# Mixer products on the un-normalised operand, weight subtractions on VectorE, and chunk decay at the state's copy

## The chip, the cores and the metric

The kernel runs on one core of a Trainium2 chip. The core has a matrix engine (TensorE, PE in the profile; its weight loads are shown as PEld), VectorE (DVE), ScalarE (ACT), GpSimd (POOL) and SyncE (SP, which here only issues transfers). Every engine works through its own queue in order and waits on semaphores for the others. Matrix products land in PSUM; all else lives in the on-chip SBUF or in DRAM. The metric is the device time of one execution in microseconds (us).

## The reference

One layer of a hybrid block on 512 tokens of width 1024, all in float32:

```python
x = x + 0.5 * swiglu(rms_norm(x, ffn1_norm), ffn1_w1, ffn1_w3, ffn1_w2)
h = rms_norm(x, mix_norm)
p = h @ w_in                       # all columns of both mixers and the gates
y_a = rwkv7_mixer(token_shift(p[rwkv columns])) @ rwkv_proj
y_b = fox_mixer(p[fox columns]) @ fox_proj
x = x + (sigmoid(g_a) * y_a + sigmoid(g_b) * y_b) @ w_out
x = x + 0.5 * swiglu(rms_norm(x, ffn2_norm), ffn2_w1, ffn2_w3, ffn2_w2)
out = rms_norm(x, final_norm)
```

`rms_norm` multiplies each token by one number, 1/sqrt(mean(x*x)+eps), and each column by a gain. The RWKV mixer is a recurrence over tokens with a 64x64 state in each of 8 heads: S_t = S_{t-1} diag(w_t) + (S_{t-1} a_t) b_t^T + v_t k_t^T, y_t = S_t r_t. The FoX mixer is causal attention with 8 heads, RMS norm of q and k per head, and a cumulative log-forget bias. The last lines of the RWKV mixer are a norm over each head (group norm), a bonus term and a gate g.

## The kernel before

**Layout.** Activations are kept transposed: 8 tiles xT of 128 columns by 512 tokens. So the normalising number of a token, rstd, is a row; it is held as a 128x512 tile, the same in every partition. Every float32 product is made from three matmuls of a split operand: each side is cut into a rounded part (hi) and a rest (lo), and hi·hi, hi·lo and lo·hi are summed in PSUM (`mm3`, L121 to L123). `cols` (L205) makes one product of 128 columns: 8 pieces of the 1024-long sum, 24 matmuls of 128x128 by 128x512.

**Weights.** `load_raw` (L100) fetches a 128-column slice with a transfer on SP's queue, into three rotating buffers. `split_w` (L107) has ScalarE round it (whi, L113) and another engine subtract (wlo, L114), each into two rotating buffers. The fifth argument picks the engine of the subtraction: VectorE where nothing is said, GpSimd where `pool` is passed. Before, `pool` is passed for the mixer's k, r and v (L471, L475, L479), q and k of FoX (L709) and the gates (L741).

**Norm.** In the feed-forward stages the operand carries only the gain and rstd is multiplied in when the product leaves PSUM (L331, L335). The mixer's first two products (psa and psg, L412, L413: low-rank codes, forget logits and the g codes) do the same (L420, L424). Then `rescale` (L196) rewrites all eight operand tiles with gain and rstd in place, splits them again, and every later product is of the normalised operand.

**Stages of the mixer.** (1) For each of four pairs of heads p, the products of k, r and v, the token shift (`shifted`, L403, a ScalarE scaling and a VectorE multiply-add), decays by a scan in chunks of 32 tokens (L484), the normalised kk with a sum over each head by a matmul (`headsum`, L130), and the operands G and BK of the chunked recurrence. GpSimd makes the products of r with the decay (L520), kk times a (L512) and BKe (L521), which is BK times the decay to the end of its chunk. (2) The inverse of a unit triangular 32x32 matrix for each of 16 chunks in each of 8 heads: 31 steps of two VectorE instructions (L569, L571). (3) A trip of its result through DRAM (Td, L572 and L578) to the layout that the recurrence needs. (4) The recurrence over 16 chunks c: xps (L622), copied as Xs (L625), ups (L629), copied into the right-hand side R (L631, L632), sps (L636), the next state, copied to the next R (L637, L638), and the output yps (L644). sps multiplies R with D, which holds BKe transposed and a diagonal block with the decay of the chunk, made by GpSimd (L610, in `stage`). Between these small products TensorE runs q and k of FoX (`load_qk`, L704), the attention and the first gates (`gate`, L739, called by `early`). (5) The group norm (L661 to L683). (6) The output projections.

**Order.** The kernel is written against tiles; a scheduler at build time orders the instructions on each engine. `holes` is written by hand: it lists matmuls of the recurrence behind which single pieces of a gate's product are put. Memory of each pool is set out by tags: a tile with the tag of another takes its place.

Of the kernel before, what the change touches and what calls it, by code (L numbers as in the profile page):

```python
# [18 lines left out]
P = 128  # L19
# [31 lines left out]
def kernel(  # L51
# [77 lines left out]

    def headsum(ps, src, hi=None, lo=None):  # L130
        hi = tmp("shi", dt=F32R)[:] if hi is None else hi
        lo = tmp("slo", dt=F32R)[:] if lo is None else lo
        dve.tensor_copy(hi, src)
        dve.tensor_tensor(lo, src, hi.bitcast(F32), op=ALU.subtract)
        pe.matmul(ps, bonesr[:], hi, start=True, stop=False)
        pe.matmul(ps, bonesr[:], lo, start=False, stop=True)
# [13 lines left out]
    class Norm:  # L150
# [36 lines left out]
        def finish(s):  # L187
# [6 lines left out]
            act.activation(s.rstd[:], ln[:], AF.Exp, scale=-0.5)  # L194

        def rescale(s, c):  # L196
            t = xT[c]
            dve.scalar_tensor_tensor(t[:], xT[c][:], pc(s.gain + c), s.rstd[:], op0=ALU.mult, op1=ALU.mult)
            hi = xp.tile([P, T], F32R, tag=f"xh{c}", name=f"xh{c}")
            lo = xp.tile([P, T], F32R, tag=f"xl{c}", name=f"xl{c}")  # L200
            act.copy(hi[:], t[:])
            (pool if c % 2 else dve).tensor_tensor(lo[:], t[:], hi[:].bitcast(F32), op=ALU.subtract)
            s.hi[c], s.lo[c] = hi, lo

# [179 lines left out]
    with ExitStack() as mx:  # L384
# [4 lines left out]
        G = [[sp.tile([P, NC, 2, C], F32, name=f"G{p}{q}", tag=f"G{p}{q}") for q in range(2)] for p in range(NP)]  # L389
        BKe = [sp.tile([P, NC, 2, C], F32, name=f"BKe{p}", tag=f"BKe{p}") for p in range(NP)]  # L390

# [25 lines left out]
        lg = rp.tile([P, T], F32, name="lg")  # L417
        fz = la
        u = tmp("u")
        dve.tensor_tensor(u[0:72, :], psa[0:72, :], mix.rstd[0:72, :], op=ALU.mult)  # L420
        shifted(la, u, 64, PAR_MUA)
        dve.tensor_scalar(fz[64:72, :], u[64:72, :], pc(PAR_F)[64:72, :], None, op0=ALU.add)
        u = tmp("u")
        dve.tensor_tensor(u[0:96, :], psg[0:96, :], mix.rstd[0:96, :], op=ALU.mult)  # L424
# [10 lines left out]
        dve.tensor_tensor(lx[q2], la[q1, :], f32(lx[q1]), op=ALU.subtract)  # L435
        zslots = [h for g in G[3] for h in (g[:, 0:8], g[:, 8:16])] + [BKe[3][:, 0:8], BKe[3][:, 8:16]]
        zslots = [h.rearrange("p c a t -> p (c a t)") for h in zslots] + spare[0:2]
# [31 lines left out]
        for p in range(NP):  # L469
            kps = bank("pk")  # L470
            mix.cols(kps[:], *load_w(win(DA + p * P), KD, P, pool), P)  # L471
            k = prep("k", p)
            shifted(k, kps, P, PAR_MU + 4 + p)
            rps = bank("pk")
            mix.cols(rps[:], *load_w(win(p * P), KD, P, pool), P)  # L475
            r = prep("r", p)
            shifted(r, rps, P, PAR_MU + p)
            vps = bank("pk")
            mix.cols(vps[:], *load_w(win(2 * DA + p * P), KD, P, pool), P)  # L479
            v = vs[p]  # L480
            shifted(v, vps, P, PAR_MU + 8 + p)

# [18 lines left out]
            ps = bank("pn", pf)  # L501
            headsum(ps[:], sq[:])
            rn = tmp("krn")
# [10 lines left out]
            dve.tensor_tensor(BK[:, :, 0, :], ch(ka), ch(Pi), op=ALU.mult)  # L514
            dve.tensor_tensor(BK[:, :, 1, :], ch(k), ch(Pi), op=ALU.mult)
            for q in range(2):
                s = slice(q * 64, (q + 1) * 64)
                dve.scalar_tensor_tensor(G[p][q][s, :, 0, :], ch(kk)[s], -1.0, Pp[s, :, 0:C],
                                         op0=ALU.mult, op1=ALU.mult)
# [70 lines left out]
        for q in range(2):  # L590
            pool.memset(Rs[0][half(q), :, q, :], 0.0)
            for i in range(4):
                o = (1 - q) * 64
                pool.memset(Rs[i][o:o + 32, :, q, :], 0.0)

        def stage(c):
            vp = pr.tile([P, NP, 2, 64], F32, tag="b", name="vp")
            for p in range(NP):
                pe.transpose(vp[0:64, p].rearrange("p a b -> p (a b)"), vs[p][:, c * C:(c + 2) * C], ident[:])
            bp = pr.tile([P, NP, 2, 64], F32, tag="b", name="bp")  # L600
            for p in range(NP):
                pe.transpose(bp[:, p].rearrange("p a b -> p (a b)"),
                             BKe[p][:, c:c + 2].rearrange("p c a b -> p (c a b)"), ident[:])
            for j in range(2):
                Rj, Dj = Rs[(c + j) % 4], Ds[(c + j) % 4]
                for q in range(2):
                    o = 32 + (1 - q) * 64
                    act.copy(Rj[o:o + 32, :, q, :], vp[j * C:(j + 1) * C, :, q, :])
                    act.copy(Dj[half(1 - q), :, q, :], bp[half(j), :, q, :])
                    pool.tensor_tensor(Dj[half(q), :, q, :],  # L610
                                       ident[half(q), half(q)].unsqueeze(1).broadcast_to([64, NP, 64]),
                                       PC[half(q), :, c + j:c + j + 1].broadcast_to([64, NP, 64]), op=ALU.mult)

        stage(0)

        for c in range(NC):
# [16 lines left out]
            if c + 1 < NC:  # L633
                sps = pr.tile([P, NP, 64], F32, tag="b", name="sps")
                for p, q in heads():
                    hs = pe.matmul(sps[half(q), p, :], Dt[:, p, q, :], R[:, p, q, :], start=True, stop=True)  # L636
                dve.tensor_copy(Rn[0:64, :, 0, :], sps[0:64])  # L637
                dve.tensor_copy(Rn[64:128, :, 1, :], sps[64:128])  # L638
            holes += [hx, hu, hu, hs]
# [12 lines left out]
        tslot = [Tall[:, i * T:(i + 1) * T] for i in range(4)]  # L652
        ya = [duo(f"BKe{p}", f"ya{p}", F32R) for p in range(NP)]
# [3 lines left out]
        nc.sync.dma_start(gup[0:96, :], rwkv_g_up[0])  # L657
        bons = gslot[12:16]
        for p in range(NP):
# [44 lines left out]
        def load_qk(p):  # L704
            both = []
            for c0, par0 in ((COL_Q, PAR_Q), (COL_KF, PAR_K)):
                o = t2.tile([P, T], F32, name=f"qk{c0}{p}")
                ps = bank("pq")
                mix.cols(ps[:], *load_w(win(c0 + p * P), KD, P, pool), P,  # L709
                         holes if 2 * p + (c0 == COL_KF) >= 7 else ())  # L710
# [3 lines left out]
                both.append((o, sq))  # L714
            for o, sq in both:
                ps = bank("pq2", pf)
                headsum(ps[:], sq[:])
# [16 lines left out]
        for b in range(NB):  # L734
            o = t2.tile([P, T], F32, name=f"vt{b}") if b else xp.tile([P, T], F32, tag="rstd", name="vt0")
# [211 lines left out]
```

## Time and profile before

| | us |
|---|---|
| median of 3 runs | 1253.06 |
| lowest, highest | 1250.62, 1253.21 |
| profiled execution | 1249.56 |
| its span, first to last instruction | 1247.5 |
| TensorE busy in the span | 1198.1 |
| VectorE, ScalarE, GpSimd busy | 673.6, 451.9, 232.6 |

The profile is of one execution. A row of a group has the line of the code, the engine, the operation, what is written and read, shapes, the count, then the time that the group kept its engine busy, the mean duration of one in nanoseconds, and the idle time of the engine right before these instructions with what ended it. A row of a stretch has its start and end, its length, and for each engine the busy time and the number of instructions. A row of a wait has who waited for whom, the total, the number of times, and the longest. A row in order of time has the start, the duration and the instruction. The clock is that granted to TensorE, 1.00 being full. Matmuls overlap with their neighbours, so the duration of one is longer than the time from one start to the next.

### The profile page before, as it was taken

How to read it: one execution, taken by the hardware profiler on the slowest of the kernel's cores; microseconds unless marked ns; L12 is line 12 of the kernel's file. 1: busy time of each engine (PE TensorE's matmuls, PEld its weight loads, DVE VectorE, ACT ScalarE, POOL GpSimd, SP SyncE). 2: the span in 40 equal slices, each digit the busy share in tenths (PEclk: the TensorE clock that was granted, in tenths of full speed). 3: DMA queues.
4: the chain of work that ended last, by engine and by line, in shares of the span. 5: the costliest groups of instructions: out<-in, count | busy, mean ns of one | idle time of the engine just before them, and what ended most of it. 6: DMA issues, size and time to landing. Idle time of an engine off the chain costs nothing.

```text
span 1247.5 us, 15857 instructions
## 1 busy us (share of the span) xinstructions
PE 1198.1 (96%) x6336; PEld 963.8 (77%) x6336; DVE 673.6 (54%) x930; ACT 451.9 (36%) x722; POOL 232.6 (19%) x202
## 2 busy tenths in 40 slices
PE   8999999999997999969889999999999999999997
PEld 6888888888884777757666777778888888888887
DVE  7544555433337788984655446487455454443332
ACT  6222222222224733436766557233322222222221
POOL 4100000001114576443221132233000000000110
PEclk9999999999998999989989999999999999999999
DMA  6233333333332233332120153543333323333332
GB/s 191 85 102 101 93 94 101 96 102 110 110 103 76 68 90 84 98 96 57 44 75 27 52 161 127 169 126 94 92 94 102 99 87 101 102 93 93 92 89 73
DMA packets 210231, 120.04 MB, mean 96 GB/s; under 512 B 11790, under 2 KB 202318, under 8 KB 210158
## 3 DMA queue, kind: packets, MB, share of 16 engines
q1 hardware_dynamic: 208382, 113.26, 31.0%
q0 software_dynamic: 1760, 5.77, 1.4%
q8 instruction: 50, 0.82, 0.3%
q14 instruction: 23, 0.19, 0.0%
q10 hardware_dynamic: 16, 0.00, 0.0%
HBM read 109.58 MB, written 9.44 MB: 95 GB/s over the span
## 4 chain that ended last, share of the span: by engine, by line
PE 84%; DVE 12%; ACT 2%; issue 1%; DMA 1%; SPq 0%; POOL 0%; DVEq 0%; ACTq 0%
PE pd L123 7%; PE pd L121 7%; PE pd L122 7%; PE pb L123 6%; PE pa L123 6%; PE pa L122 6%; PE pa L121 6%; PE pb L122 6%; PE pb L121 6%; PE pgt L121 3%; PE pgt L122 2%; PE pgt L123 2%; DVE prod L569 2%; PE pk L122 1%; PE pw L123 1%
## 5 line engine op out<-in xcount | busy, mean ns | idle before, releaser
L113 ACT CAST whi<-raw 128x1024 fp32r<-128x1024 f32 (+3 forms) x199 | 198.3, 997 | 629.0 <-PE pa L122 178.8
L114 DVE TENSOR_TENSOR wlo<-raw,whi 128x1024 fp32r<-128x1024 f32 (+2 forms) x162 | 192.7, 1190 | 115.9 <-ACT whi L113 113.9
L123 PE MATMUL pb<-xh,wlo 128*128 128x512 f32 x344 | 134.1, 390 | 0.9 <-DVE wlo L114 0.9
L121 PE MATMUL pa<-xh,whi 128*128 128x512 f32 x344 | 134.8, 392 | 0.0
L121 PE MATMUL pb<-xh,whi 128*128 128x512 f32 x344 | 134.4, 391 | 0.0
L123 PE MATMUL pa<-xh,wlo 128*128 128x512 f32 x344 | 134.1, 390 | 0.0
L122 PE MATMUL pa<-xl,whi 128*128 128x512 f32 x344 | 134.0, 390 | 0.0
L122 PE MATMUL pb<-xl,whi 128*128 128x512 f32 x344 | 134.0, 390 | 0.0
L123 PE MATMUL pd<-hh,wlo 128*128 128x512 f32 x330 | 131.3, 398 | 0.0
L121 PE MATMUL pd<-hh,whi 128*128 128x512 f32 x330 | 130.4, 395 | 0.0
L122 PE MATMUL pd<-hl,whi 128*128 128x512 f32 x330 | 130.4, 395 | 0.0
L114 POOL TENSOR_TENSOR wlo<-raw,whi 128x1024 fp32r<-128x1024 f32 x37 | 91.6, 2475 | 125.4 <-ACT whi L113 123.6
L335 DVE TENSOR_TENSOR fb<-pb,rstd 128x512 f32<-128x512 f32 x43 | 29.7, 691 | 137.2 <-PE pb L123 137.2
L123 PEld LDWEIGHTS pb<-xh,wlo 128*128 128x128 f32 x344 | 64.6, 188 | 14.7 <-DVE wlo L114 1.3
L121 PEld LDWEIGHTS pa<-xh,whi 128*128 128x128 f32 x344 | 64.6, 188 | 13.8 <-issue 0.5
L122 PEld LDWEIGHTS pb<-xl,whi 128*128 128x128 f32 x344 | 64.6, 188 | 13.6 <-issue 0.2
L121 PEld LDWEIGHTS pb<-xh,whi 128*128 128x128 f32 x344 | 64.6, 188 | 13.7 <-ACT whi L113 0.3
L122 PEld LDWEIGHTS pa<-xl,whi 128*128 128x128 f32 x344 | 64.6, 188 | 13.6 <-issue 0.2
L123 PEld LDWEIGHTS pa<-xh,wlo 128*128 128x128 f32 x344 | 64.6, 188 | 13.4
L899 POOL TENSOR_TENSOR facc<-facc,osq 128x512 f32<-128x512 f32 x6 | 10.1, 1676 | 346.6 <-ACT osq L898 346.6
L122 PEld LDWEIGHTS pd<-hl,whi 128*128 128x128 f32 x330 | 62.0, 188 | 14.9
L123 PEld LDWEIGHTS pd<-hh,wlo 128*128 128x128 f32 x330 | 62.0, 188 | 14.8 <-issue 0.2
(359 smaller groups left out, 2154.1 us busy)
## 6 DMA issues: line engine op xcount, KB each, us to landing
raw<-in_ffn_w_dram SPq DMA_DIRECT2D x118, 512.0 KB
raw<-in_w_in_dram SPq DMA_DIRECT2D x40, 512.0 KB
raw<-in_ffn_w_dram SPq DMA_DIRECT2D x15, 384.0 KB
raw<-in_w_out_dram SPq DMA_DIRECT2D x8, 512.0 KB
gsave<-gs SPq DMA_DIRECT2D x12, 256.0 KB
xin<-in_x_dram SPq DMA_DIRECT2D x4, 512.0 KB
xsave<-xT POOLq DMA_DIRECT2D x8, 256.0 KB, 2.3
ga<-gsave SPq DMA_DIRECT2D x8, 256.0 KB
```

Of the source, the lines that this page charges most:

```text
L113: act.copy(hi[:], raw[:])
L114: (eng or dve).tensor_tensor(lo[:], raw[:], hi[:].bitcast(F32), op=ALU.subtract)
L121: pe.matmul(ps, whi, xhi, start=first, stop=False)
L122: pe.matmul(ps, whi, xlo, start=False, stop=False)
L123: pe.matmul(ps, wlo, xhi, start=False, stop=last)
L335: dve.tensor_tensor(b[:], pb[:], nrm.rstd[:], op=ALU.mult)
L569: dve.tensor_tensor(pv, TT[:, 0:n, t:t + 1].broadcast_to([P, n, m]), Lu[:, t, n:C].unsqueeze(1).broadcast_to([P, n, m]), op=ALU.mult)
L899: pool.tensor_tensor(acc[:], acc[:], sq[:], op=ALU.add)
```

## The change

Six things change; the rest follows from them.

1. `rescale` goes. All products of the mixer are of the operand with the gain alone. A product is multiplied by rstd on VectorE as it leaves PSUM: k, r and v in a new function `normed`, q and k of FoX and the gates in place. The attention's v has its tokens in partitions, so it needs rstd as a column: four transposes of rstd give `rc`, and ScalarE's copy of v takes it as a scale. The gain of q and k moves to the last multiplication of these.
2. The weight subtractions of the mixer that were on GpSimd are on VectorE.
3. kk times a and the products of r with the decay move from GpSimd to VectorE.
4. BKe goes. The transposes in `stage` read BK itself, which is kept for all four p; the diagonal block of D is a plain identity, written once; and the decay of the chunk is multiplied into the state by VectorE as it leaves PSUM, in place of two copies.
5. `headsum` takes its rounded part from ScalarE for the norms of k (RWKV) and of q and k (FoX).
6. rstd stays alive longer, so v's first tile has a place of its own, and the g codes (lg) are a temporary tile that is stored to DRAM and fetched again in the group norm.

```diff
-    def headsum(ps, src, hi=None, lo=None):
+    def headsum(ps, src, hi=None, lo=None, eng=None):
...
-        dve.tensor_copy(hi, src)
+        if eng is act:
+            act.copy(hi, src)
+        else:
+            dve.tensor_copy(hi, src)
...
-        def rescale(s, c):
-            t = xT[c]
-            dve.scalar_tensor_tensor(t[:], xT[c][:], pc(s.gain + c), s.rstd[:], op0=ALU.mult, op1=ALU.mult)
...
-            act.copy(hi[:], t[:])
-            (pool if c % 2 else dve).tensor_tensor(lo[:], t[:], hi[:].bitcast(F32), op=ALU.subtract)
...
-        for c in range(KD):
-            mix.rescale(c)
+        rc = rp.tile([P, NB], F32, name="rc")
+        rps = bank("rct", pr)
+        for b in range(NB):
+            pe.transpose(rps[:, b * P:(b + 1) * P], mix.rstd[:, b * P:(b + 1) * P], ident[:])
+        dve.tensor_copy(rc[:], rps[:, 0:T:P])
...
+        def normed(ps, rows=P):
+            u = tmp("u")
+            dve.tensor_tensor(u[0:rows, :], ps[0:rows, :], mix.rstd[0:rows, :], op=ALU.mult)
+            return u
...
+        nc.sync.dma_start(lgsave[:], lg[0:96, :])
...
-            mix.cols(kps[:], *load_w(win(DA + p * P), KD, P, pool), P)
+            mix.cols(kps[:], *load_w(win(DA + p * P), KD, P), P)
             k = prep("k", p)
-            shifted(k, kps, P, PAR_MU + 4 + p)
+            shifted(k, normed(kps), P, PAR_MU + 4 + p)
...
-            headsum(ps[:], sq[:])
+            headsum(ps[:], sq[:], eng=act)
...
-            pool.tensor_tensor(ka[:], kk[:], a[:], op=ALU.mult)
-            BK = t2.tile([P, NC, 2, C], F32, name="BK", tag="BK", bufs=2)
+            dve.tensor_tensor(ka[:], kk[:], a[:], op=ALU.mult)
+            BK = BKs[p]
...
-                pool.tensor_tensor(G[p][q][s, :, 1, :], ch(r)[s], Pp[s, :, 1:C + 1], op=ALU.mult)
-            pool.tensor_tensor(BKe[p][:].rearrange("p c a t -> p c (a t)"),
-                              BK[:].rearrange("p c a t -> p c (a t)"),
-                              Pp[:, :, C:C + 1].broadcast_to([P, NC, 2 * C]), op=ALU.mult)
+                dve.tensor_tensor(G[p][q][s, :, 1, :], ch(r)[s], Pp[s, :, 1:C + 1], op=ALU.mult)
...
+                pool.tensor_copy(Ds[i][half(q), :, q, :],
+                                 ident[half(q), half(q)].unsqueeze(1).broadcast_to([64, NP, 64]))
...
-                    pool.tensor_tensor(Dj[half(q), :, q, :],
-                                       ident[half(q), half(q)].unsqueeze(1).broadcast_to([64, NP, 64]),
-                                       PC[half(q), :, c + j:c + j + 1].broadcast_to([64, NP, 64]), op=ALU.mult)
...
-                dve.tensor_copy(Rn[0:64, :, 0, :], sps[0:64])
-                dve.tensor_copy(Rn[64:128, :, 1, :], sps[64:128])
+                for q in range(2):
+                    dve.tensor_tensor(Rn[half(q), :, q, :], sps[half(q)],
+                                      PC[half(q), :, c:c + 1].broadcast_to([64, NP, 64]), op=ALU.mult)
...
+        nc.sync.dma_start(lg[0:96, :], lgsave[:])
...
+                dve.tensor_tensor(o[:], ps[:], mix.rstd[:], op=ALU.mult)
                 sq = tmp("qsq")
-                act.activation(sq[:], ps[:], AF.Square)
-                act.activation(o[:], ps[:], AF.Copy, scale=pc(par0))
+                act.activation(sq[:], o[:], AF.Square)
...
-                dve.tensor_tensor(o[:], o[:], rn[:], op=ALU.mult)
+                dve.scalar_tensor_tensor(o[:], o[:], pc(par0), rn[:], op0=ALU.mult, op1=ALU.mult)
...
-            act.copy(o[:], vps[b][:])
+            act.activation(o[:], vps[b][:], AF.Copy, scale=rc[:, b:b + 1])
...
-            mix.cols(ps[:], *load_w(win(c0 + m * P), KD, P, pool), P, holes)
-            act.activation(g, ps[:], AF.Tanh, scale=0.5)
+            mix.cols(ps[:], *load_w(win(c0 + m * P), KD, P), P, holes)
+            dve.tensor_tensor(g, ps[:], mix.rstd[:], op=ALU.mult)
+            act.activation(g, g, AF.Tanh, scale=0.5)
```

More of the change, by code (lines that the diff above doesn't have):

```diff
@@ L389 @@
         G = [[sp.tile([P, NC, 2, C], F32, name=f"G{p}{q}", tag=f"G{p}{q}") for q in range(2)] for p in range(NP)]
-        BKe = [sp.tile([P, NC, 2, C], F32, name=f"BKe{p}", tag=f"BKe{p}") for p in range(NP)]
+        BKs = [sp.tile([P, NC, 2, C], F32, name=f"BK{p}", tag=f"BK{p}") for p in range(NP)]
         def duo(tag, name, dt=F32):
@@ L602, in stage @@
                 pe.transpose(bp[:, p].rearrange("p a b -> p (a b)"),
-                             BKe[p][:, c:c + 2].rearrange("p c a b -> p (c a b)"), ident[:])
+                             BKs[p][:, c:c + 2].rearrange("p c a b -> p (c a b)"), ident[:])
             for j in range(2):
@@ L652 @@
         tslot = [Tall[:, i * T:(i + 1) * T] for i in range(4)]
-        ya = [duo(f"BKe{p}", f"ya{p}", F32R) for p in range(NP)]
+        ya = [duo(f"BK{p}", f"ya{p}", F32R) for p in range(NP)]
         ya = [[t[:, i] for i in range(2)] for t in ya]
@@ L708, in load_qk @@
                 ps = bank("pq")
-                mix.cols(ps[:], *load_w(win(c0 + p * P), KD, P, pool), P,
+                mix.cols(ps[:], *load_w(win(c0 + p * P), KD, P), P,
                          holes if 2 * p + (c0 == COL_KF) >= 7 else ())
+                dve.tensor_tensor(o[:], ps[:], mix.rstd[:], op=ALU.mult)
                 sq = tmp("qsq")
-                act.activation(sq[:], ps[:], AF.Square)
-                act.activation(o[:], ps[:], AF.Copy, scale=pc(par0))
-                both.append((o, sq))
-            for o, sq in both:
+                act.activation(sq[:], o[:], AF.Square)
+                both.append((o, sq, par0))
+            for o, sq, par0 in both:
                 ps = bank("pq2", pf)
-                headsum(ps[:], sq[:])
+                headsum(ps[:], sq[:], eng=act)
                 rn = tmp("qrn")
@@ L734 @@
         for b in range(NB):
-            o = t2.tile([P, T], F32, name=f"vt{b}") if b else xp.tile([P, T], F32, tag="rstd", name="vt0")
-            act.copy(o[:], vps[b][:])
+            o = t2.tile([P, T], F32, name=f"vt{b}")
+            act.activation(o[:], vps[b][:], AF.Copy, scale=rc[:, b:b + 1])
             vt.append(o)
```

23 lines of the change are left out of this document (10 added, 13 removed).

## The prediction

> **What bounds the kernel now.** I read the page first (shares and totals), then the busy time by stage, then the groups of each stage, the waits, and last the order of time where a group's mean was odd. TensorE decides the whole:
>
> ```profile
> span 1247.5 us, 15857 instructions
> ...
> PE 1198.1 (96%) x6336; PEld 963.8 (77%) x6336; DVE 673.6 (54%) x930; ACT 451.9 (36%) x722; POOL 232.6 (19%) x202
> ```
>
> TensorE is idle for 49 us of 1247.5, so only idle time, and time at a lowered clock, can be won. The change acts between 386.7 us (the mixer's reciprocal norm is ready) and 800 us. Stage by stage (length, then busy time of each engine, clock, DMA share, GB/s):
>
> ```profile
> core 0: us, PE busy (x) PEld busy (x) DVE busy (x) ACT busy (x) POOL busy (x), PEclk, DMA share, GB/s
> 386.70:515.80 129.10, 113.39 (x677) 89.31 (x676) 108.68 (x113) 63.27 (x94) 79.96 (x67) 0.96 0.28 78
> 515.80:552.50 36.70, 30.63 (x132) 24.04 (x130) 34.77 (x69) 12.70 (x19) 12.32 (x6) 1.00 0.31 86
> 552.50:568.00 15.50, 11.18 (x42) 8.88 (x42) 9.31 (x12) 7.09 (x11) 9.39 (x11) 0.78 0.45 103
> 568.00:720.00 152.00, 141.51 (x1464) 106.77 (x1464) 81.24 (x189) 99.83 (x265) 36.72 (x33) 0.96 0.17 51
> 720.00:775.00 55.00, 53.08 (x247) 41.27 (x247) 29.32 (x37) 37.79 (x52) 19.63 (x8) 0.97 0.50 158
> 775.00:800.00 25.00, 25.00 (x109) 19.97 (x108) 12.22 (x19) 6.31 (x12) 4.95 (x9) 1.00 0.56 181
> ```
>
> They are: (1) preparation of the RWKV operands; (2) the triangular inverse, a chain of 62 VectorE instructions; (3) its trip through DRAM up to the first step of the recurrence; (4) 16 recurrence steps woven with attention and gates; (5) group norm; (6) output projections. In (1) and (2) VectorE is busy for 108.7 of 129.1 and 34.8 of 36.7 us: it sets the end there. From (4) on TensorE is busy 93% and more. The last row also prices a matmul: 25.00/109 = 0.229 us. Two waits of TensorE are large:
>
> ```profile
> PE pq L135 <- DVE shi L133: 10.4, 3, 6.7
> ...
> PE pk L121 <- ACT xh L201: 8.1, 1, 8.1
> ```
>
> The first is VectorE being late with the head sums of q and k, the second the rescaling of the operand. Why VectorE is slow is seen inside the inverse:
>
> ```profile
> 518.01 0.30 DVE L569 TENSOR_TENSOR prod<-TT,Ls 128x135 f32<-128x135 f32 x1
> ...
> 518.35 0.30 DVE L571 TENSOR_TENSOR TT<-TT,prod 128x135 f32<-128x135 f32 x1
> ...
> 518.64 2.39 POOL L114 TENSOR_TENSOR wlo<-raw,whi 128x1024 fp32r<-128x1024 f32 x1 [5.58 <-ACT whi L113]
> 518.68 2.53 DVE L569 TENSOR_TENSOR prod<-TT,Ls 128x156 f32<-128x156 f32 x1
> ...
> 521.25 0.32 DVE L571 TENSOR_TENSOR TT<-TT,prod 128x156 f32<-128x156 f32 x1
> ```
>
> An instruction worth 0.32 us takes 2.53 us because GpSimd began a 2.39 us subtraction 0.04 us earlier: it stands still for all of it. [...] The same in stage 1, as groups (count, busy us, mean ns, idle before):
>
> ```profile
> L198 DVE SCALAR_TENSOR_TENSOR xT<-xT,par,rstd 128x512 f32<-128x512 f32 x8 | 11.6, 1524 | 4.8 <-ACT rstd L194 4.8
> L543 DVE TENSOR_TENSOR G<-gp,gmask 64x512 f32<-64x512 f32 x16 | 11.0, 688 | 0.4
> L134 DVE TENSOR_TENSOR slo<-ksq,shi 128x512 fp32r<-128x512 f32 x4 | 7.0, 1752 | 0.1
> L114 DVE TENSOR_TENSOR wlo<-raw,whi 128x1024 fp32r<-128x1024 f32 x4 | 4.9, 1221 | 1.0 <-ACT whi L113 1.0
> L518 DVE SCALAR_TENSOR_TENSOR G<-Tall 64x512 f32<-64x512 f32 x4 | 4.8, 1188 | 0.1
> L518 DVE SCALAR_TENSOR_TENSOR G<-kk,Pp 64x512 f32<-64x512 f32 x4 | 4.7, 1180 | 0.1
> L202 DVE TENSOR_TENSOR xl<-xT,xh 128x512 fp32r<-128x512 f32 x4 | 4.2, 1072 | 0.0
> ...
> L133 DVE CAST shi<-ksq 128x512 fp32r<-128x512 f32 x4 | 4.2, 1039 | 2.0 <-ACT ksq L500 2.0
> L525 DVE SCALAR_TENSOR_TENSOR rk<-r,par,k 128x512 f32<-128x512 f32 x2 | 3.8, 1902 | 0.0
> L514 DVE TENSOR_TENSOR BK<-kka,Tall 128x512 f32<-128x512 f32 x2 | 3.6, 1778 | 0.0
> L525 DVE SCALAR_TENSOR_TENSOR rk<-spare,par 128x512 f32<-128x512 f32 x2 | 3.5, 1768 | 0.0
> L405 DVE SCALAR_TENSOR_TENSOR spare<-pk,par,spare 128x511 f32<-128x511 f32 x4 | 3.0, 746 | 9.5 <-ACT spare L404 9.5
> ...
> L515 DVE TENSOR_TENSOR BK<-spare,Tall 128x512 f32<-128x512 f32 x2 | 2.9, 1461 | 0.0
> ```
>
> **The change, stage by stage.** Prices of operations outside stage 1:
>
> ```profile
> L114 POOL TENSOR_TENSOR wlo<-raw,whi 128x1024 fp32r<-128x1024 f32 x37 | 91.6, 2475 | 125.4 <-ACT whi L113 123.6 <-PE lp L790 1.6
> ...
> L335 DVE TENSOR_TENSOR fb<-pb,rstd 128x512 f32<-128x512 f32 x43 | 29.7, 691 | 137.2 <-PE pb L123 137.2
> ...
> L610 POOL TENSOR_TENSOR RD<-ident,PC 64x256 f32<-64x256 f32 x32 | 21.7, 677 | 75.3 <-PE sps L636 65.5 <-PE yps L644 7.9 <-DVE rk L525 0.6
> ...
> L142 DVE CAST hh<-fh 128x512 fp32r<-128x512 f32 x44 | 18.5, 421 | 0.1
> ...
> L637 DVE COPY RD<-sps 64x256 f32<-64x256 f32 x15 | 6.2, 415 | 23.5 <-PE sps L636 23.4
> ```
>
> A weight subtraction costs 1.221 us on VectorE against 2.475 on GpSimd; 36 of the 37 move. A product scaled as it leaves PSUM (ps times rstd) is the form of L335: 0.691. An undisturbed two-input form of 512 columns is 0.688 (L543), one with a scalar 0.746 (L405), a cast 0.421 (L142).
>
> Stage 1. Blocked time per group is count x (mean less undisturbed price): L198 6.2, L134 4.3, L518 1.8+1.7, L202 1.5, L133 2.5, L525 2.3+2.0, L514 2.2, L515 1.5, together 26.0 us. GpSimd keeps only memsets and small copies, so I take it as gone. VectorE loses: the whole of L198 (8 x 1.524 = 12.2) and L202 (4 x 1.072 = 4.3), the four casts of the head sums, which go to ScalarE (4 x 0.421 = 1.7), and the blocked time of the other groups (18.3): 36.5. It gains 12 weight subtractions (14.7), 12 scalings (8.3), the r halves of G (8 x 0.688 = 5.5) and four products kk times a (2.8): 31.3. So 108.7 becomes 103.5 us. Its idle time was 129.1-108.7 = 20.4 us. TensorE's wait of 8.1 goes, since no product waits for the rescaling, and GpSimd's answers are waited for no more, which shortens it; but the new order of the changed program's instructions (an order without times) puts nearly all filling work ahead of the last masked products, so the transfer of L to the inverse lies bare. I bound the idle by 8 and 20: the stage takes 111 to 124, a gain of 5 to 18, taken at 11. The four transposes for the token-wise norm start after the rest of that norm, on TensorE, some 0.229 each at most: inside that bound. ScalarE gains 4 casts and loses 8 of the operand (63 of 129 us busy): nothing. The store of lg stands in SP's queue behind a sigmoid, and weight loads behind it; the three raw buffers hold products for 3 x 24 x 0.229 = 16 us ahead, so nothing; if that cover went, the delay is one load.
>
> Stage 2. Five GpSimd subtractions fall into it, each blocking about 2.53-0.32 = 2.2 us: -11.0; two casts leave, -0.8. By the new order eight subtractions (9.8), six scalings of q and k (4.1) and eight more steps of q and k (about 4 x 0.421, 3 x 0.688, 0.746 = 4.5) stand inside the chain, and some 20 more steps between instructions at about 0.04 (518.35 from 518.01+0.30): 0.8. Sum +7.4; taken +8, bounds +5 and +10. This stage loses: the blocking was cheaper than the work that takes its place, because that work is also pulled ahead.
>
> Stage 3. The inverse goes out and in on GpSimd's queue:
>
> ```profile
> 553.47 0.58 POOL L572 DMA_DIRECT2D Td<-TT  x1
> 554.14 2.33 POOL L114 TENSOR_TENSOR wlo<-raw,whi 128x1024 fp32r<-128x1024 f32 x1
> 556.69 3.17 POOL L578 DMA_DIRECT2D Tall<-Td  x4 [0.21 <-issue]
> ```
>
> ```profile
> Td<-TT POOLq DMA_DIRECT2D x1, 512.0 KB, 2.9
> Tall<-Td POOLq DMA_DIRECT2D x4, 128.0 KB, 5.2
> ```
>
> 553.47+2.9 = 556.4, so the subtraction between them costs 0.3 only; the last load lands near 559.1+5.2 = 564.3, yet the step starts at 568, behind products of q and k in TensorE's order. In the new order 171 of the 192 such matmuls stand ahead of that step instead of 135, done while VectorE ran the longer inverse. So the step starts when the load lands: -3 (bounds 0, -4), and 36 x 0.229 = 8.2 us of TensorE's work no longer follow it. Where the steps are bound by their own chain that frees nothing; taken -6 (bounds 0, -8).
>
> Stage 4. VectorE gains nine subtractions (11.0), six scalings of gates (4.1) and two of q and k (1.4), and loses six casts (2.5): +14.0 on 81.2 of 152, less blocking. For the 30 state copies (0.415) now with the decay: from below 0.415, from above 0.688 for a row twice as wide, so 0 to +8.2; taken 0, the same elements from the same PSUM. GpSimd's 32 decay products (0.677) go, replaced by eight copies made once while it is free. VectorE was idle for 71 us here: taken 0, bounds -6 and +13.
>
> Stage 5. Seven subtractions (8.5) and ten scalings (6.9) on an engine busy 29.3 of 55, while TensorE has 1.9 idle: taken -1, bounds -3 and +3.
>
> Sum: -11+8-3-6+0-1 = -13. Against the profiled execution (1249.56 us, 2.06 of it outside the span) that is 1236.6; the median shown is 1253.06, 3.5 higher, and from it the forecast is **1240**.
>
> **Rivals.** *VectorE becomes the bound of the recurrence* (slower). Its queue is in order: a subtraction of 1.221 and a scaling of 0.691 ahead of the copy of a state holds the next step. If everything added in stage 4 (16.5) and the wider price of the decay (up to 8.2) falls on the steps, with no blocking to win back, it is +21 or so: 1240+21 = 1261. It decides from 13 of these on. For it: TensorE waits for VectorE in stage 2 and 3. Against: 71 us idle. Chance 0.22.
>
> *TensorE is set free throughout* (faster). Its idle time in stages 1 to 5 is 15.7+6.1+4.3+10.5+1.9 = 38.5 us, and the lowered clock cost 0.04x129.1+0.22x15.5+0.04x152+0.03x55 = 16.4. If half of both goes, -27: 1226. [...] Chance 0.17.
>
> *Nothing is won.* VectorE's work in stage 1 comes as late as before, gaining 3, the inverse loses 8, stage 3 and the matmuls ahead return 5: 1253. Chance 0.08.
>
> **How the numbers follow.** The forecast has 0.53; its own range is 1230 to 1250 by the bounds of stages 1, 2 and 4 not all falling one way. A change under 0.2% (2.5 us) can't be told from none here: same 0.08, faster 0.53+0.17 = 0.70, slower 0.22. The range runs from 1224, below the freer case, to 1258, into the slower one.
>
> **What would show it.** Right: no wait of TensorE near 391 us; the groups L134, L518, L525 at 0.69 to 0.75; inverse near 505 us, 44 to 46 long; TensorE idle some 10 us before the first step, about 563. Wrong: an inverse that starts after 512, or recurrence steps that wait for subtractions, with VectorE above 70% there.

## The result, and the profile after

The changed kernel takes 1263.65 us (median of 4 runs, 1262.24 to 1264.96), the kernel before 1252.34 on the same chip: ratio 1.0092, 95% interval 1.0074 to 1.0109. It is slower by 11 us, 0.9%; 1240 was forecast. The profiled execution took 1264.96 us. Its page and its mean clock, and the mean clock of before:

```profile
span 1262.9 us, 15874 instructions
...
PE 1215.6 (96%) x6340; PEld 978.5 (77%) x6340; DVE 670.3 (53%) x991; ACT 451.0 (36%) x718; POOL 98.1 (8%) x122
```

```profile
core 0: 1262.9 us, clock 0.969
```

```profile
core 0: 1247.5 us, clock 0.984
```

TensorE is idle for 1262.9-1215.6 = 47.3 us, 2 less than before (49.4). What its lowered clock costs is (1-clock) x span: 39.1 us, where it was 20.0. So 19 us went into the clock and nowhere else. The stages of after, cut at the same events as before (norm ready; first instruction of the inverse; its last; first step of the recurrence; last Xs; first output projection, which before stands at 780.1 us and not at the 775 of the earlier rows):

```profile
core 0: us, PE busy (x) PEld busy (x) DVE busy (x) ACT busy (x) POOL busy (x), PEclk, DMA share, GB/s
386.70:534.20 147.50, 130.64 (x685) 103.42 (x684) 98.48 (x133) 62.76 (x92) 18.02 (x35) 0.84 0.25 71
534.20:578.70 44.50, 44.50 (x197) 36.68 (x196) 40.75 (x90) 20.05 (x29) 0.18 (x1) 1.00 0.32 90
578.70:588.30 9.60, 4.24 (x16) 2.64 (x15) 5.42 (x9) 6.39 (x11) 4.59 (x9) 0.88 0.76 218
588.30:732.60 144.30, 133.29 (x1416) 99.92 (x1417) 80.26 (x192) 92.41 (x253) 0.00 (x0) 0.94 0.15 46
732.60:795.00 62.40, 59.74 (x275) 46.31 (x275) 39.73 (x63) 39.89 (x56) 2.80 (x6) 0.97 0.45 141
```

The whole loss is in stage 1: 147.5 us against 129.1, at a clock of 0.84 against 0.96. There (1-0.84) x 147.5 = 23.6 and 0.04 x 129.1 = 5.2 us are lost: the difference, 18.4, is the whole lengthening. Where the clock is lowered, by stretches:

```profile
425.60:439.30 13.70, 12.34 (x77) 9.77 (x77) 9.29 (x14) 3.92 (x6) 1.52 (x4) 0.50 0.23 66
439.30:456.30 17.00, 14.74 (x65) 11.83 (x63) 9.70 (x14) 6.30 (x9) 0.44 (x2) 1.00 0.22 62
456.30:470.00 13.70, 13.12 (x78) 10.43 (x79) 9.70 (x14) 3.70 (x6) 2.29 (x3) 0.50 0.24 68
...
487.00:500.70 13.70, 13.53 (x79) 10.75 (x80) 10.92 (x15) 2.67 (x4) 3.84 (x6) 0.50 0.24 69
```

A cycle of 30.7 us, one for each of the first three pairs of heads, runs 13.7 us of it at half rate. What starts it is seen in the order of time, on TensorE and then on VectorE:

```profile
450.44 0.39 PE L139 MATMUL pn<-slo,bonesr 128*128 128x512 f32 x1
...
453.65 0.39 PE L123 MATMUL pk<-xh,wlo 128*128 128x512 f32 x1
456.88 2.08 PE L526 MATMUL pn<-rk,bones 128*128 128x512 f32 x2 [2.83 <-DVE rk L524]
```

```profile
450.87 0.69 DVE L506 TENSOR_SCALAR krn<-pn 128x512 f32<-128x512 f32 x1 [0.66 <-PE pn L139]
...
454.66 1.38 DVE L520 SCALAR_TENSOR_TENSOR G<-kk,Pp 64x512 f32<-64x512 f32 x2
456.07 0.75 DVE L524 SCALAR_TENSOR_TENSOR rk<-r,par,k 128x512 f32<-128x512 f32 x1
```

Behind the head sum (L139, 450.44) VectorE's queue holds nine instructions, from krn to the bonus row rk. Krn waits for the head sum, and the others stand behind krn. The row itself needs only r and k, not the head sum, but it is the last of the nine; the small products behind it need G, and a BK (L516) that comes after the row. The nine take 6.0 us, to 456.82. TensorE's queue holds 14 matmuls between the head sum and the bonus product (L526): 3.2 us of work. So TensorE stands idle for 2.83 us (5.05 in the first pair), drops to half rate, and runs the bonus product and the 64 small products of G with BK at that rate: the 64 take 5.99 us, where in the kernel before the second pair's took 3.40 at the full clock. In the kernel before 42 to 46 matmuls, some 10 us at 0.229 each, stood in this place, and the bonus row was waited for in the last pair alone:

```profile
PE pn L527 <- DVE rk L525: 3.0, 1, 3.0
```

After the drop VectorE waits in its turn for the slowed products of v (a matmul every 0.43 us from 465.4 on, every 0.23 from 470.1 on); the waits of after (three of the five waits for a product are such, 16.2 of the 21.4 us):

```profile
DVE u L419 <- PE pk L123: 21.4, 5, 5.9
...
PE pn L526 <- DVE rk L524: 16.9, 4, 6.2
```

### The profile page after: what moved, and what is told of

Its sections match the earlier page's. It is cut to its first block, busy times and chain, and to the rows that moved or that the text cites. A ratio compares the mean times of both kernels' runs of the same rounds, so it can differ in the third digit from the quotient of the medians.

```text
span 1262.9 us, 15874 instructions
## 1 busy us (share of the span) xinstructions
PE 1215.6 (96%) x6340; PEld 978.5 (77%) x6340; DVE 670.3 (53%) x991; ACT 451.0 (36%) x718; POOL 98.1 (8%) x122
## 3 DMA queue, kind: packets, MB, share of 16 engines
q1 hardware_dynamic: 208606, 113.65, 30.7%
## 4 chain that ended last, share of the span: by engine, by line
PE 87%; DVE 6%; issue 3%; DMA 1%; ACT 1%; POOL 1%; SPq 0%; DVEq 0%; POOLq 0%; ACTq 0%
PE pd L122 7%; PE pd L121 7%; PE pd L123 7%; PE pb L123 6%; PE pa L123 6%; PE pa L121 6%; PE pa L122 6%; PE pb L121 6%; PE pb L122 6%; PE pgt L121 3%; PE pgt L123 2%; PE pgt L122 2%; DVE wlo L114 2%; PE gp L539 2%; PE pw L123 1%
## 5 line engine op out<-in xcount | busy, mean ns | idle before, releaser
L114 DVE TENSOR_TENSOR wlo<-raw,whi 128x1024 fp32r<-128x1024 f32 (+2 forms) x198 | 236.9, 1197 | 129.9 <-ACT whi L113 127.7
L123 PEld LDWEIGHTS pb<-xh,wlo 128*128 128x128 f32 x344 | 64.6, 188 | 15.2 <-DVE wlo L114 1.6
L122 PEld LDWEIGHTS pa<-xl,whi 128*128 128x128 f32 x344 | 64.6, 188 | 13.7 <-issue 0.2
L121 PEld LDWEIGHTS pd<-hh,whi 128*128 128x128 f32 x330 | 62.0, 188 | 14.9 <-issue 0.2
L325 DVE TENSOR_TENSOR fa<-pa,rstd 128x512 f32<-128x512 f32 x43 | 29.7, 691 | 73.2 <-PE pa L123 72.9
```

The source lines that it names most:

```text
L114: (eng or dve).tensor_tensor(lo[:], raw[:], hi[:].bitcast(F32), op=ALU.subtract)
L121: pe.matmul(ps, whi, xhi, start=first, stop=False)
L122: pe.matmul(ps, whi, xlo, start=False, stop=False)
L123: pe.matmul(ps, wlo, xhi, start=False, stop=last)
L325: dve.tensor_tensor(a[:], pa[:], nrm.rstd[:], op=ALU.mult)
```

## The experiments

The theory after this reading: the change moves the head sum late in TensorE's order, TensorE waits, and the clock that it loses there is the loss. Rivals: VectorE is late because of the subtractions it took over; the engines take turns and the clock is only a sign of it; the scaling itself, not the order, makes the row late. All kernels, with the matmuls of k, r and v that TensorE's order has between head sum and bonus product (pairs 0, 1, 2; the last pair, which has only products of the attention's v there, or none, is left out), and of the profiled execution TensorE's idle time, the clock's loss, and the rest of the span. Each ratio is to runs of the kernel before on the same chip (medians 1251.60 to 1252.34):

| kernel | between | idle | clock | rest | median us | ratio to before |
|---|---|---|---|---|---|---|
| before | 46, 44, 42 | 49.4 | 20.0 | 1178.1 | 1252.34 | |
| after | 10, 14, 14 | 47.3 | 39.1 | 1176.5 | 1263.65 | 1.0092 |
| subs_only | 56, 45, 39 | 43.0 | 19.8 | 1176.8 | 1240.85 | 0.9914 (0.9898 to 0.9931) |
| scale_back | 57, 46, 46 | 42.7 | 22.4 | 1176.9 | 1244.76 | 0.9947 (0.9928 to 0.9965) |
| subs_back | 1, 14, 14 | 54.5 | 38.0 | 1175.8 | 1267.76 | 1.0129 (1.0113 to 1.0145) |
| decay_only | 46, 45, 45 | 48.8 | 23.7 | 1176.0 | 1250.20 | 0.9987 (0.9977 to 0.9996) |
| subs_decay | 56, 45, 39 | 45.5 | 18.6 | 1176.7 | 1242.52 | 0.9927 (0.9912 to 0.9942) |
| head_late | 12, 12, 12 | 50.4 | 34.0 | 1176.3 | 1263.08 | 1.0094 (1.0070 to 1.0117) |
| late_v | 34, 38, 38 | 51.1 | 26.3 | 1175.5 | 1256.37 | 1.0040 (1.0027 to 1.0054) |
| gp_late | 10, 14, 14 | 49.7 | 26.3 | 1175.6 | 1253.52 | 1.0018 (1.0003 to 1.0032) |
| fill10 | 10, 14, 21 | 40.0 | 17.4 | 1188.8 | 1248.42 | 0.9981 (0.9969 to 0.9993) |
| fill_pin | 10, 14, 14 | 42.5 | 27.6 | 1185.5 | 1259.27 | 1.0069 (1.0045 to 1.0093) |
| fill_behind | 10, 14, 14 | 45.1 | 23.9 | 1186.8 | 1257.83 | 1.0049 (1.0031 to 1.0067) |
| subs_gp1 | 57, 55, 27 | 47.6 | 28.8 | 1176.4 | 1255.82 | 1.0030 (1.0019 to 1.0040) |
| subs_gp1_fill | 57, 55, 27 | 40.2 | 19.9 | 1186.7 | 1248.56 | 0.9960 (0.9945 to 0.9976) |
| subs_fill | 56, 45, 39 | 37.6 | 17.4 | 1186.6 | 1243.97 | 0.9939 (0.9917 to 0.9961) |

The rest is the same within 3 us in all eleven kernels without added matmuls (1175.5 to 1178.1), whatever VectorE and GpSimd have to do: it is about TensorE's work at the full clock (idle time at half rate is counted in both sums). Only idle time and the clock tell these kernels apart.

**The subtractions alone** (subs_only), on the kernel before, for k, r, v, q, k of FoX and the gates:

```diff
-            mix.cols(kps[:], *load_w(win(DA + p * P), KD, P, pool), P)
+            mix.cols(kps[:], *load_w(win(DA + p * P), KD, P), P)
```

> The kernel before with one part of the change alone: the weight subtractions of the mixer (k, r, v, the attention's q and k, the gates) on VectorE instead of GpSimd; the operand is still normalised. Two theories of the lost 18 us in operand preparation. Theory A (the scaling of the products on VectorE moved the head sum late in TensorE's order, to some 14 products ahead of the bonus product where it stood 44 ahead, so TensorE waits there and its clock halves): here the head sum stands 39 to 56 products ahead, no wait for the bonus row over 1 us, operand preparation at 115 to 130 us with a granted clock of at least 0.95, total 1240 to 1250 us. Theory B (the moved subtractions, 12 of 1.2 us, make VectorE late): operand preparation at 140 us or more and clock 0.84 to 0.88, total 1258 us or more.

1240.85 us: the fastest of all, 11 us under the kernel before. The moved subtractions are not what makes VectorE late. Details of the expectation were off: stage 1 took 131.9 us at a clock of 0.92, since TensorE still waits for the rescaled operand at its start and for the bonus row once, in the last pair:

```profile
PE pn L527 <- DVE rk L525: 8.0, 1, 8.0
PE pk L121 <- ACT xh L201: 3.9, 1, 3.9
```

**The normalised operand put back into the changed kernel** (scale_back):

```diff
+        for c in range(KD):
+            mix.rescale(c)
...
-            shifted(k, normed(kps), P, PAR_MU + 4 + p)
+            shifted(k, kps, P, PAR_MU + 4 + p)
...
```

> The changed kernel with the normalised operand put back (rescaled ahead of the products; no scaling behind them), the subtractions still on VectorE and the decay still applied as the state leaves PSUM. Theory A: head sum 57 to 72 products ahead of the bonus product, so no wait there over 1 us; the wait for the rescaled operand of about 8 us comes back ahead of the first product; operand preparation from the first product on no longer than 125 us, clock at least 0.95, total 1240 to 1250 us. Theory B (VectorE late because of the moved subtractions, ka and half of G): still 1258 us or more, clock 0.84 to 0.88 in operand preparation.

1244.76 us; the head sum is early again and the bonus row is waited for in the last pair alone, which the expectation did not have:

```profile
PE pn L532 <- DVE rk L530: 6.4, 1, 6.4
```

**The subtractions given back to GpSimd** (subs_back), the mirror image: the first diff backwards, on the changed kernel.

> The changed kernel with the mixer's weight subtractions given back to GpSimd; the products stay un-normalised and are scaled behind. TensorE's written order has the head sum only 1 to 14 products ahead of the bonus product. Theory A (the scaling behind the products is what moved the head sum late): the waits for the bonus row stay, three or four of them over 2 us, clock at most 0.90 in operand preparation, which takes 145 us or more; blocking of VectorE comes back on top; total 1262 to 1280 us. Theory B (the moved subtractions make VectorE late): operand preparation falls to 130 us or less, total 1250 us or less.

1267.76 us, with four waits for the bonus row:

```profile
PE pn L526 <- DVE rk L524: 21.6, 4, 7.7
```

Together the three runs put the lateness on the scaling behind the products; the subtractions are a gain with it and without it (1267.76 to 1263.65; 1251.60 to 1240.85).

**Fillers ahead of the bonus product** (fill10): ten matmuls whose result is overwritten. Bonus and small products are also held behind the r product of the next pair, where TensorE's order of the changed kernel has them.

```diff
             ps = bank("pn", pf)
+            for _ in range(10):
+                pe.matmul(ps[:], bonesr[:], mix.hi[0][:], start=True, stop=True)
             pe.matmul(ps[:], bones[:], rk[:], start=True, stop=True)
```

> The changed kernel with ten 128x512 matmuls into the bonus product's own bank, ahead of each bonus product (overwritten by it), the order of everything else on TensorE as it was within a few products. Theory C (the clock is the loss: TensorE waits 3 to 5 us, drops to half rate and the small products behind don't bring it back): the half-rate stretches near 426, 456 and 487 us go, operand preparation at 130 to 135 us, total 1246 to 1252 us. Theory D (TensorE and VectorE take turns, the clock is only a sign of it): the fillers use the same wait and operand preparation stays at 145 to 150 us, or up to 13 us longer, total 1262 us or more.

1248.42 us: 40 added matmuls make the changed kernel 15 us faster. From the norm to the inverse the clock is full:

```profile
391.80:515.10 123.30, 119.62 (x723) 96.20 (x722) 95.99 (x130) 61.31 (x90) 16.66 (x35) 1.00 0.33 88
```

But the scheduler had also put 18 to 24 products of v ahead of the small products. In the last pair it had put 29 products of the attention's v between head sum and bonus product, so that the 6.2 us of wait there went without a filler. Three more kernels take this apart.

**The same fillers, written behind the small products** (fill_behind):

```diff
                         pe.matmul(gp[o, c], BK[s, cc], G[p][q][s, cc], start=True, stop=True)
+                if g:
+                    ps = bank("pn", pf)
+                    for _ in range(10):
+                        mf = pe.matmul(ps[:], bonesr[:], mix.hi[0][:], start=True, stop=True)
```

> The control of the fillers: the changed kernel with the same ten 128x512 matmuls per pair, but behind the 64 small products instead of ahead of the bonus product, so that they come after the wait. Theory C (the wait itself lowers the clock): waits and half-rate stretches near 426, 456 and 487 us stay and the fillers run at half rate, operand preparation 147 to 160 us, total 1262 to 1277 us. If any dense stretch of large matmuls near that place repaired the clock, whatever its place: 1255 us or less.

TensorE's order had the fillers right behind the bonus product, with 8 to 13 products of v behind them and then the small ones. 1257.83 us is in neither range: the waits stayed to the digit (16.9 us, 4 times), but the half-rate stretches shrank from 13.7, 13.7 and 13.7 to 6.8, 6.8 and 3.4 us.

**Fillers with TensorE's order held as in the changed kernel** (fill_pin): as fill10, and

```diff
+            with tc.issue_after(mix.gl.ins) if late else ExitStack():
                 mix.cols(vps[:], *load_w(win(2 * DA + p * P), KD, P), P)
```

with mix.gl the last small product of the pair before.

> The ten fillers ahead of each bonus product as in fill10, but with the 64 small products held directly behind the bonus product (in fill10 they had come 18 to 24 products later), so that TensorE's order is that of the changed kernel and only the fillers are added. Theory C (the wait lowers the clock, the fillers hold it): no half-rate stretch between 420 and 505 us, 120 to 128 us from the first product to the inverse, total 1246 to 1251 us. If the gain of fill10 came from the later place of the small products: half-rate stretches are back and the total is 1256 us or more.

1259.27 us, in the range of the rival: of fill10's gain of 15.2 us 4.4 are left, so most of it, 10.9 us, hung on the place of the small products. The fillers hold the clock in the second pair (no drop), not in the first, where 2.72 us of wait are left behind them, and there the stretch lasts 10.2 us. In the third pair only 0.47 us of that wait are left, but the small products then wait 1.72 us for BK, and the clock drops for 6.8 us from 486.3 on. In the last pair 28 products of the attention's v stand between, as in fill10, so even the 4.4 us are not the fillers' alone.

**The small products later, no fillers** (gp_late): the 64 small products of pair p behind 18 of the 24 matmuls of the next v.

> No fillers: the changed kernel with the bonus product where it was and the 64 small products of pairs 0 to 2 held behind 18 products of the next v. If the wait sets the drop of the clock and the work behind it the length of the drop (large products bring it back, small ones don't): the waits of 5.1, 2.8 and 2.8 us stay, the half-rate stretches shrink from 13.7 to about 6.8 us each, which gives 3 x 6.8/2 = 10 us, total 1252 to 1256 us. If the place of the small products doesn't matter: 1261 us or more; if it was all of fill10's gain: 1250 us or less.

1253.52 us, in the range, but not by the stretches expected: 6.8 us behind the first wait, none behind the second and 3.4 behind the third. The waits are as in the changed kernel (16.8 us, 4 times):

```profile
424.50:431.30 6.80, 3.95 (x7) 2.49 (x8) 5.99 (x10) 3.70 (x6) 0.34 (x2) 0.50 0.29 77
431.30:479.10 47.80, 42.17 (x277) 33.90 (x276) 35.44 (x50) 16.77 (x24) 3.34 (x9) 1.00 0.26 72
479.10:482.50 3.40, 3.40 (x10) 2.63 (x9) 3.40 (x5) 1.03 (x3) 1.92 (x2) 0.50 0.40 113
```

So what stands behind a wait makes the length of the drop. In the changed kernel the clock came back 4.4, 5.2 and 5.6 us after the large products behind the small ones began, and not during 6.0 us of dense 64x64 ones; here it came back 3.9 us after the first bonus product began (427.4 to 431.3). And a wait makes the drop, but not every wait of one length: it matters where it falls. In the traces of before and after every change of the clock lies on a grid of 3.41 us, and the three stretches above are 2, 14 and 1 cells of such a grid. In the changed kernel the second wait, 2.83 us, leaves 1.13 us of TensorE's work in the cell of the grid ahead of the drop (452.91 to 456.32). Here the same wait falls across two cells, which keep 2.45 and 1.54 us of work, and the clock stays full. In the traces of before and after half rate follows every cell at the full clock with up to 1.49 us of work, and none with 2.05 us or more; between the two both are seen.

**The bonus product and the small products behind the next v** (late_v):

```diff
             mix.cols(vps[:], *load_w(win(2 * DA + p * P), KD, P), P)
+            if late:
+                with tc.issue_after(mix.end.ins):
+                    finish(*late)
```

> The changed kernel with the bonus product and the 64 small products of pair p queued on TensorE behind the v product of pair p+1 (24 products later than before; for the last pair nothing changes). Theories A and C: the wait for the bonus row goes, clock at least 0.95 in operand preparation, which takes 125 to 133 us; total 1245 to 1251 us. Theory B (VectorE itself is late): VectorE is just as late with the last pair, operand preparation 142 us or more whatever TensorE's clock, total 1258 us or more.

1256.37 us, outside both ranges, though stage 1 falls from 147.5 to 135.6 us. The wait for the bonus row goes but for the last pair; another takes its place, for the PSUM bank that VectorE's scaling still has to read:

```profile
PE pk L121 <- DVE u L419: 12.8, 3, 5.7
PE pn L473 <- DVE rk L557: 6.2, 1, 6.2
```

Here the rival that the engines take turns has its share. What the scaling costs with the early order of before held on TensorE was not run.

**The late order without the scaling** (head_late): subs_only with the changed kernel's order pinned on TensorE, the head sum in the middle of the next r, the bonus and small products before the next v.

```diff
+            for kd in range(KD):
+                mix.end = mm3(rps[:], rw[0][:, kd], rw[1][:, kd], ...)
+                if late and kd == 3:
+                    with tc.issue_after(mix.end.ins):
+                        hps = head(late[1])
...
+                with tc.issue_after(mix.end.ins):
+                    finish(lp, *got)
```

> The kernel before with the weight subtractions alone on VectorE (1240.9 us; no scaling behind the products), and on TensorE the order of the changed kernel pinned: the head sum of pair p behind 12 matmuls of the r product of the next pair, its bonus product and small products 12 matmuls later, before the next v product. If the order alone loses the time: waits for the bonus row of 2.5 us or more in each pair, half-rate stretches of some 13 us each, 138 to 148 us from the first product to the inverse, total 1255 to 1268 us. If it takes the extra scalings on VectorE as well: waits under 2 us, no half-rate stretch between 425 and 490 us, total 1238 to 1247 us.

1263.08 us, in the first range: 22 us lost against subs_only by the order, with no scaling on VectorE. The same drops, at the same spacing:

```profile
437.80:451.50 13.70, 12.36 (x76) 9.77 (x77) 8.90 (x12) 1.95 (x3) 6.42 (x7) 0.50 0.27 68
451.50:468.50 17.00, 14.76 (x65) 11.83 (x63) 8.62 (x11) 7.41 (x10) 1.65 (x1) 1.00 0.22 62
468.50:482.20 13.70, 11.98 (x76) 9.44 (x77) 9.34 (x12) 1.95 (x3) 6.40 (x8) 0.50 0.26 68
...
499.20:512.90 13.70, 11.27 (x74) 8.94 (x75) 10.21 (x13) 0.72 (x1) 8.82 (x8) 0.50 0.19 59
```

```profile
PE pn L502 <- DVE rk L497: 12.6, 4, 3.7
```

**The decay alone, and with the subtractions** (decay_only, subs_decay):

```diff
...
-                dve.tensor_copy(Rn[0:64, :, 0, :], sps[0:64])
-                dve.tensor_copy(Rn[64:128, :, 1, :], sps[64:128])
+                for q in range(2):
+                    dve.tensor_tensor(Rn[half(q), :, q, :], sps[half(q)],
+                                      PC[half(q), :, c:c + 1].broadcast_to([64, NP, 64]), op=ALU.mult)
...
```

> The kernel before with the third part alone: the chunk decay applied as the state leaves PSUM, on VectorE, and no decay products on GpSimd. Operand preparation loses four blocking GpSimd operations (0 to 6 us shorter); the recurrence loses 28 decay products on GpSimd: if the wide price of the scaled copy counts on the steps, they are up to 8 us longer and the total is 1252 to 1258 us; if blocking counts, 2 to 6 us shorter, total 1243 to 1249 us. Taken: 1249 us.

> The kernel before with the second and the third part, the subtractions and the decay, and the operand normalised as before. By the run with the subtractions alone (1240.9 us) and if the decay's worth is the same with them: 1237 to 1241 us; if the decay's worth was only that GpSimd blocks less, which the subtractions have taken already: 1241 to 1245 us. Head sum 39 to 56 products ahead of the bonus product, so no wait for the bonus row but the last pair's.

1250.20 us, 0.1% under the kernel before and between the ranges, and 1242.52, no better than 1240.85 and in the second range: the decay is worth next to nothing by itself and nothing beside the subtractions.

**The last pair** (subs_gp1, subs_gp1_fill, subs_fill), on subs_only: the bonus product of every pair pinned behind its small products; this with thirty fillers behind the last head sum; the fillers alone.

> The kernel before with the weight subtractions alone on VectorE (1240.9 us), and the bonus row and its product moved behind the 64 small products of the same pair: in the last pair the small products, which the inverse waits for, came behind a wait of 8.0 us for the bonus row and 2.1 us of its product at half rate. If that lies on the path: the inverse begins 2 to 4 us earlier, total 1237 to 1239 us. If the small products wait just as long for the last G: 1240 to 1243 us.

> The same with thirty 128x512 matmuls behind the head sum of the last pair, in the wait that is left there (30 x 0.23 = 6.9 us), so that the small products of that pair run at the full clock (3.4 us instead of 5.9). Expected 2 to 3 us less than the run without them, 1235 to 1238 us. If the fillers end after the last G is ready, they are in the way: 1240 us or more.

> The kernel before with the weight subtractions alone on VectorE, and thirty 128x512 matmuls behind the head sum of the last pair, where TensorE waits 8.0 us for the last bonus row and then runs the bonus product and the 64 small products at half rate. If the clock in that wait is on the path: the bonus product takes 1.1 us and the small products 3.4 us instead of 2.1 and 5.9, the inverse begins 3 to 4 us earlier, total 1236 to 1239 us. If the transfer to the inverse waits for something else: 1240 to 1243 us.

None gave the gain expected. Pinned, the small products of the last pair wait 7.8 us themselves, for the last BK:

```profile
PE gp L531 <- DVE BK L514: 7.8, 1, 7.8
```

The clock is halved for 20.5 us from 498.5 on, and 15 us are lost, 1255.82, outside both ranges. The fillers give 7.3 us of it back (half rate 3.4 us), more than the 2 to 3 expected, but 1248.56 is no gain on subs_only. On subs_only itself they save 5.4 us of idle time and 2.4 of the clock, but are work of their own: the inverse begins 1.3 us earlier (517.3 against 518.6 us) and the time is 1243.97, 3 us longer (the intervals of the two ratios overlap). The price of 5.9 us for the small products was wrong there: in subs_only 17 products of the attention's v stand ahead of them, and they run at the full clock already, in 3.4 us from 508.3 on. Against subs_only the pinned order costs 4.6 us of idle time and 9.0 of the clock; why the last BK is so late in it was not taken further.

## Why the prediction was wrong

It failed at one term of the sum, stage 1: "I bound the idle by 8 and 20: the stage takes 111 to 124, a gain of 5 to 18, taken at 11". Measured: +18.4; the inverse starts at 534.2 us, and a start after 512 was the sign of being wrong. The first half of that term held. No product waits for a rescaled operand (the first came at 391.9 instead of 399.1 us), the blocking is gone, and VectorE's groups have the prices given:

```profile
L419 DVE TENSOR_TENSOR u<-pk,rstd 128x512 f32<-128x512 f32 x12 | 8.0, 684 | 21.4 <-PE pk L123 21.4
...
L137 DVE TENSOR_TENSOR slo<-ksq,shi 128x512 fp32r<-128x512 f32 x4 | 2.7, 685 | 0.0
```

Head sum parts at 685 ns, 1752 before. VectorE's busy time fell from 108.7 to 98.5 us (103.5 forecast). But its idle time, bounded at 20, became 49.0. The bound assumed that VectorE sets the end of the stage, so that less work on it means an earlier end. The stage is a loop through both engines, and the account of the table shows that TensorE's idle time and clock decide. The term took TensorE's wait of 8.1 us away and put new waits and the clock at nothing: measured are 16.9 us of waits for the bonus row, and a clock that costs 23.6 us in the stage instead of 5.2. The new order was used for stages 2 and 3, but not for the number of matmuls that cover VectorE between head sum and bonus product: 14 x 0.229 = 3.2 us for nine instructions of about 0.69, 6.2 us. Both follow from the order and the rows of before; the size of the clock's loss does not. With the clock held (fill10) VectorE's idle time is still 128.4-99.0 = 29.4 us, but the 40 fillers are up to 40 x 0.229 = 9.2 us of that stage; whether the bound of 20 would have held without the loss of clock is not shown.

The rival on the faster side let half of TensorE's idle time and half of the clock's loss go, -27. That half was the author's estimate, and no run shows it: in the changed kernel idle time went from 49.4 to 47.3 us, and the clock's loss rose from 20.0 to 39.1, through new waits.

The other terms, by the stages above (before, after):

- Stage 2, +8: 36.7 to 44.5 us, +7.8. Right.
- Stage 3, -3: 15.5 to 9.6, -5.9. Right in sign, beyond the bound of -4; TensorE is idle 5.4 us there, where about 10 were foretold.
- The matmuls done ahead, -6, and stage 4, 0: 152.0 to 144.3, -7.7. Right, and 171 of the 192 matmuls stand ahead of the first step, as counted.
- Stage 5, -1: from the last Xs to the first output projection 60.1 to 62.6, +2.5. Wrong in sign, inside the bound of +3.

Stages 2 to 5 together were forecast at -2 and measured at -3.3 (264.3 to 261.0 us). A shorter inverse is not worth its own difference, though: scale_back has one of 35.3 us where the changed kernel has 44.5, and comes from its start to the projections in 259.4 us, 1.6 less than the changed kernel, not 9.

The rival on the slower side gave 1261 us, near the result, but by luck: its own terms, 16.5+8.2 = 24.7, were entered as 21, and the recurrence got shorter, not longer, with small waits for VectorE:

```profile
PE ups L627 <- DVE Xs L623: 9.1, 5, 3.8
```

The forecast of 1240 is met by the kernel with the subtractions alone, 1240.85, but that too is luck. Its stage 1 is 2.8 us longer than before, not 11 shorter (131.9 against 129.1). It gains behind that: 253.4 against 264.3 us from the start of the inverse to the projections, where the wait for the head sums of q and k falls from 10.4 us in all to 2.0:

```profile
PE pq L135 <- DVE shi L133: 2.0, 1, 2.0
```

## What to carry to other kernels

Before pricing an engine's work by the stage, make the account of the engine that is 96% busy: its idle time, plus (1-clock) x span; here these two explained the eleven kernels without added matmuls within 3 us. Where work leaves that engine for another and comes back, hold what its queue has in between against the time away, in the new order: in the changed kernel waits of 2.81 to 5.05 us, with small products behind them, cost half of 13.7 us each in clock alone. And take a bundled change apart: one of its parts alone beats both kernels.

## What the hardware did that was not expected

- In the changed kernel waits of 2.81 and 2.83 us halved the clock, with 0.73 and 1.13 us of work left in the 3.41 us ahead of the drop. But a wait of 2.83 us in gp_late (ending at 453.6) and one of 3.52 us in late_v (ending at 481.9) did not halve it, and of two waits of 2.72 us the one in fill10 did not and the one in fill_pin did.
- The lengths of the half-rate stretches are 3.4, 6.8, 10.2, 13.7 and 20.5 us, multiples of 3.4, and the cycle of 30.7 us is nine of them.
- A dense run of 64 matmuls of 64x64 (6.0 us, 458.9 to 464.9) did not bring the clock back; 5.2 us of large ones behind it did. Whether their size or their spacing decides was not tried.
